# A hybrid decoder trunk on one core: the closing seven-product group of three SwiGLUs takes five blocks instead of four

## The chip, the cores and the metric

The kernel runs on one core of a Trainium2 chip. The core has a matrix engine (TensorE, here PE), a vector engine (VectorE, DVE), an activation engine (ScalarE, ACT), GpSimd (POOL) and a synchronisation engine (SyncE, SP). In this kernel SP and POOL issue nearly all of the DMA transfers, which the core's 16 DMA engines carry out. The metric is the time of one execution in microseconds (us).

## The reference

Two layers work on one sequence of 512 tokens with model width 1024, all in float32. Each layer has a SwiGLU, a mixing part (sliding-window attention beside a short convolution, with one combined input and one output projection) and a second SwiGLU. What matters here are the four SwiGLUs:

```python
D_MODEL = 1024
SEQ = 512
DEPTH = 2
D_FF = 2816
...
def swiglu(h, w_gate, w_up, w_down):
    return (jax.nn.silu(h @ w_gate) * (h @ w_up)) @ w_down
...
    for l in range(DEPTH):
        x = x + 0.5 * swiglu(rms_norm(x, ffn1_norm[l]), ffn1_wg[l], ffn1_wu[l], ffn1_wd[l])
        h = rms_norm(x, mix_norm[l])
        ...
        x = x + jnp.concatenate([attn_out, conv_out], axis=-1) @ w_out[l]
        x = x + 0.5 * swiglu(rms_norm(x, ffn2_norm[l]), ffn2_wg[l], ffn2_wu[l], ffn2_wd[l])
    return rms_norm(x, final_norm)
```

The down product (`@ w_down`) has the hidden width 2816 as its inner dimension, 1024 columns and 512 rows of tokens.

## The kernel before

**Precision.** Each float32 operand is split into a rounded part and what is left: `hi` is a cast on ACT (line 221), `lo = raw - hi` a subtraction on DVE (line 222), both in the type that PE multiplies at full rate. A product takes three matmuls: hi x hi, lo x hi, hi x lo. Weights arrive by DMA as tiles `raw_n` of two rows of 128 x 512 (shape 128 x 2 x 512, called 128x1024 in the profile, 512 KB) and become `wh_n` and `wl_n`. There are 8 buffers for raw tiles and 4 each for `wh` and `wl`; `take_split` asks for the split of the tile three ahead (`SPLIT_AHEAD`), and each split asks for a load four tiles further on (`LOAD_AHEAD`). Both wait for the buffer that comes round.

**A SwiGLU in blocks.** The hidden width is 11 blocks of 256. A list of stages tells in which order gate, up and down products are done: `p` and `w` make activations of one or two blocks, `u` those of block 10, `d` is a plain down product of the blocks named, `s` a group. The lists are `FIRST` (first SwiGLU of layer 0), `INNER` (second of layer 0, first of layer 1) and `LAST` (second of layer 1).

**A plain block** (`down`, line 383) multiplies one block's activations with its 2 weight rows: 4 row pieces of 128 tokens, 2 column halves of 512, 2 inner rows of 128, 3 matmuls each, so 48 matmuls of 128x512. Its results are added into the residual `x` by DVE (line 1372) or go on in banks that a group left open. In `INNER` the last two blocks have their own routine, `down_end` (line 422), which also feeds the next norm and takes one weight tile in other room (`wx`).

**A group** (`s`) takes four blocks and does seven products where plain multiplication has eight, after the seven-product scheme for 2 x 2 block matrices. Three objects take part:

- `plan` (function `seven`) puts ten weight tiles of the four blocks in line, some loaded with a second one added on top by an accumulating DMA that POOL issues, and orders seven forms of them (`FORMS`, or `EARLY` for the group at an end). Sums of tiles are made in `need_split`: on DVE as raw<-raw (line 249) or as a DMA of POOL (line 277).
- `Seven` makes the operands from the activations: b11, b21, b22 are the raw blocks (`fb..` tiles, 128x1024), t1 to t4 sums of them (`ft..` tiles). Each is split on ACT and DVE, but names listed in `far` take `split_far`: ACT writes the negative of the raw tile (line 227) and the rounded part (line 228), and POOL adds the raw tile by DMA (line 229).
- `share` runs the seven steps; a step is 2 weight tiles times 12 matmuls, so a group has 7 x 24 = 168. The accumulators are called x, y, w and z, here `x_s`, `y_s`, `w_s`, `z_s`, and go into `x` on DVE (line 1005).

The operands of the second group are made inside the steps of the first. `share` with `after` is the form for an end: it also drives the next norm, whose transposes (`xt`, line 705) stand between the last products.

**What sets the order.** A scheduler puts the instructions of each engine in a row; each engine works through its row in order and waits by semaphores. POOL issues its DMAs in order too, so what stands behind a waiting one waits with it. At the ends PE's row is written by hand (`by_hand`).

Of the kernel before, what the change touches and what calls it, by code (L numbers as in the profile page):

```python
# [8 lines left out]
F32 = mybir.dt.float32  # L9
# [7 lines left out]
P = 128  # L17
D = 1024
S = 512
# [50 lines left out]
    ((1, 1, -1), (0, 1, 1)), ((0, 1, 1),),  # L70
)
# [4 lines left out]
def trunk_kernel(  # L76
# [154 lines left out]
    def need_split(g):  # L231
        while state["split"] <= min(g, len(order) - 1):
# [3 lines left out]
            if what in (None, "wide", "room", "far"):  # L236
                need_raw(u if far else u + LOAD_AHEAD)
                raw = raw_of.pop(u)
            elif isinstance(what, tuple):

                what, h, how = what
                far = how == "far"
                last = {"a11": 0, "a12": 4, "s2": 2, "s3": 6, "s1": 2, "a22": 8, "s4": 4}[what]
                need_raw(u + h if far else u + max(last, 4) + h + LOAD_AHEAD)
                a11, s1, a12, s3, a22 = (raw_of.get(u + 2 * i + h) for i in range(5))
                if what == "s2":
                    late = state["late"] if h else None
                    with tc.issue_after(late) if late else nullcontext():
                        nc.vector.tensor_add(a11, a11, s1)  # L249
# [14 lines left out]
            if what == "room":  # L264
                hi, lo = both(f"wx_{n}", shape=(P, 2, 2, S))
            else:
                hi = wpool.tile(shape, F32R, tag="wh", bufs=4, name=f"wh_{n}")
                lo = wpool.tile(shape, F32R, tag="wl", bufs=4, name=f"wl_{n}")
# [4 lines left out]
            if isinstance(order[n][1], tuple):  # L273
# [13 lines left out]
                for i in done:  # L287
                    del raw_of[u + 2 * i + h]
            split_of[n] = (hi, lo)
            state["split"] += 1  # L290
            if far:

                with tc.issue_after(sent.ins):
                    need_raw(u + LOAD_AHEAD + (4 + h if isinstance(order[n][1], tuple) else 0))
# [110 lines left out]
    def down_end(acts, blocks, norm, open_):  # L405

        a, b = blocks
        held = []

        def tile_of(n):  # L410
            while len(held) <= n:
                held.append(take_split(min(SPLIT_AHEAD, 4 - len(held)))[1:])
            return held[n]

        def products(acc, t, n):
            tok = slice(t * P, (t + 1) * P)
# [1397 lines left out]
```

## Time and profile before

| what | us |
| --- | --- |
| median of 3 runs | 1635.62 |
| lowest and highest | 1635.52, 1637.23 |
| profiled execution | 1635.43 |
| its span | 1633.7 |
| PE busy | 1624.8 (99%) |
| DVE busy | 1304.0 (80%) |
| ACT busy | 1142.0 (70%) |
| POOL busy | 192.1 (12%) |

The span is the time from the first to the last record of the execution. Engines work side by side, so their busy times don't add up. In the rows of groups the columns are line, engine, operation, out<-in by the program's names, shape and count, then busy us in all and mean ns of one, then idle time before it and what ended it. In the table of stages each stretch is from:to in us, with the busy time of every engine, the granted clock of TensorE, the busy share of the 16 DMA engines and GB/s. The weight loads of the first SwiGLU's last three stages lie between 244 and 338 us.

### The profile page before, as it was taken

The page shows a single profiled execution, that of the slowest core. Times are in us where ns is not written, and L with a number is a line of the kernel's source. Part 1 is how long each engine was busy: PE and PEld are TensorE (multiplying, and loading weights), DVE is VectorE, ACT ScalarE, POOL GpSimd, SP SyncE. Part 2 cuts the span into 40 slices and gives each one's busy share as a digit, 9 for nine tenths or more (in the row PEclk, how much of TensorE's full clock was granted, in tenths as well). Part 3 has the DMA queues.
Part 4 walks back from the last instruction along what each step waited for, and adds up shares of the span by engine and source line. Part 5 has one row for each costly group of instructions (what it writes and reads, how often), then busy time and mean ns, then how long its engine had stood idle before and what let it go on. Part 6 is the DMA issues. An engine that isn't in the chain of part 4 may idle for free.

```text
span 1633.7 us, 21063 instructions
## 1 busy us (share of the span) xinstructions
PE 1624.8 (99%) x7544; PEld 1353.7 (83%) x7544; DVE 1304.0 (80%) x1718; ACT 1142.0 (70%) x1597; POOL 192.1 (12%) x172
## 2 busy tenths in 40 slices
PE   9999999999999999999999999999999999999998
PEld 7888888898888888888888888888988888888886
DVE  7987779878899867789688667887678987778885
ACT  7457777558867677786476777865597775777864
POOL 0011111100120111112001111110002101111111
PEclk9999999999999999999999999999999999999999
DMA  9379999934685788999737888997147857899992
GB/s 258 88 196 220 222 224 251 219 90 88 177 200 129 206 207 218 210 235 254 217 82 202 211 211 220 234 246 199 45 108 196 202 132 196 215 213 234 222 248 84
DMA packets 295292, 310.74 MB, mean 190 GB/s; under 512 B 116980, under 2 KB 179476, under 8 KB 295188
## 3 DMA queue, kind: packets, MB, share of 16 engines
q1 hardware_dynamic: 252660, 230.09, 48.7%
q0 software_dynamic: 41824, 78.65, 28.3%
q8 instruction: 59, 0.97, 0.2%
q10 hardware_dynamic: 704, 0.66, 0.1%
q14 instruction: 45, 0.37, 0.1%
HBM read 263.74 MB, written 2.10 MB: 163 GB/s over the span
## 4 chain that ended last, share of the span: by engine, by line
PE 93%; ACT 5%; DVE 1%; DMA 1%; issue 1%; SPq 0%; ACTq 0%; DVEq 0%
PE x L961 25%; PE y L961 13%; PE x_s L961 10%; PE w L961 6%; PE y_s L961 5%; PE up L1118 4%; PE down L383 3%; PE w_s L961 3%; PE acc L313 3%; PE acc L314 3%; PE acc L316 2%; PE acc L360 2%; PE x_m L961 1%; PE xt L705 1%; PE y_m L961 1%; ACT p L1589 1%
## 5 line engine op out<-in xcount | busy, mean ns | idle before, releaser
L222 DVE TENSOR_TENSOR wl<-raw,wh 128x1024 fp32r<-128x1024 f32 (+1 forms) x493 | 599.2, 1221 | 211.3 <-ACT wh L221 204.8
L221 ACT CAST wh<-raw 128x1024 fp32r<-128x1024 f32 (+1 forms) x493 | 511.7, 1044 | 300.3 <-PE y L961 37.5
L961 PE MATMUL x<-wh,ft 128*128 128x512 f32 x608 | 187.2, 389 | 0.0
L961 PE MATMUL y<-wh,ft 128*128 128x512 f32 x608 | 187.1, 389 | 0.0
L961 PE MATMUL x<-wh,fb 128*128 128x512 f32 x608 | 187.1, 389 | 0.0
L961 PEld LDWEIGHTS x<-wh,ft 128*128 128x128 f32 x608 | 114.2, 188 | 23.7
L961 PEld LDWEIGHTS x<-wh,fb 128*128 128x128 f32 x608 | 114.2, 188 | 23.7
L961 PEld LDWEIGHTS y<-wh,ft 128*128 128x128 f32 x608 | 114.1, 188 | 23.7
L961 PE MATMUL x<-wl,fb 128*128 128x512 f32 x304 | 118.3, 389 | 0.0
L961 PE MATMUL x<-wl,ft 128*128 128x512 f32 x304 | 118.3, 389 | 0.0
L961 PE MATMUL y<-wl,ft 128*128 128x512 f32 x304 | 118.3, 389 | 0.0
L1287 ACT COPY raw_a<-pt 128x1024 uint16<-128x1024 uint16 x76 | 103.3, 1360 | 17.9 <-DMA pt<-pl 17.8
L216 POOL DMA_DIRECT2D raw<-in_ffn_wu_dram x39 | 47.0, 1208 | 546.3 <-DMA raw<-in_ffn_wu_dram 351.4
L313 PE MATMUL acc<-hh,wh 128*128 128x512 f32 x240 | 94.0, 392 | 0.0
L961 PE MATMUL w<-wh,fb 128*128 128x512 f32 x304 | 93.6, 389 | 0.0
L314 PE MATMUL acc<-hl,wh 128*128 128x512 f32 x240 | 93.5, 390 | 0.0
L316 PE MATMUL acc<-hh,wl 128*128 128x512 f32 x240 | 93.4, 389 | 0.0
L961 PE MATMUL y_s<-wh,ft_s 128*128 128x512 f32 x256 | 78.8, 389 | 0.0
L961 PE MATMUL x_s<-wh,ft_s 128*128 128x512 f32 x256 | 78.8, 389 | 0.0
L249 DVE TENSOR_TENSOR raw<-raw,raw 128x1024 f32<-128x1024 f32 x58 | 70.5, 1219 | 9.1 <-DMA raw<-in_ffn_wd_dram 6.0
L216 POOL DMA_DIRECT2D raw<-in_ffn_wg_dram x39 | 46.8, 1206 | 235.2 <-DMA raw<-in_ffn_wu_dram 88.4
L961 PE MATMUL x_s<-wh,fb_s 128*128 128x512 f32 x240 | 74.0, 389 | 0.2 <-DVE x L1005 0.2
(370 smaller groups left out, 3431.7 us busy)
## 6 DMA issues: line engine op xcount, KB each, us to landing
raw<-in_ffn_wu_dram SPq DMA_DIRECT2D x120, 512.0 KB, 5.1
raw<-in_ffn_wd_dram SPq DMA_DIRECT2D x104, 512.0 KB, 6.9
raw<-in_ffn_wg_dram SPq DMA_DIRECT2D x80, 512.0 KB, 5.4
raw<-in_ffn_wu_dram POOLq DMA_DIRECT2D x39, 512.0 KB, 8.4
raw<-in_ffn_wg_dram POOLq DMA_DIRECT2D x39, 512.0 KB, 5.9
raw<-in_w_in_dram SPq DMA_DIRECT2D x36, 512.0 KB, 4.5
raw<-in_ffn_wd_dram POOLq DMA_DIRECT2D x32, 512.0 KB, 8.6
raw<-raw POOLq DMA_DIRECT2D x20, 512.0 KB, 8.9
```

What stands on the lines that cost most here:

```text
L216: nc.gpsimd.dma_start(out=r, in_=rows_of(*more), accum_op=ALU.add)
L221: cast = nc.scalar.copy(hi, raw)
L222: state["sub"] = eng.tensor_sub(lo, raw, f32(hi))
L249: nc.vector.tensor_add(a11, a11, s1)
L313: nc.tensor.matmul(acc, hi[:, k, :], rhs[k][0], start=k == first, stop=False)
L314: nc.tensor.matmul(acc, hi[:, k, :], rhs[k][1], start=False, stop=False)
L316: state["product"] = nc.tensor.matmul(acc, lo[:, k, :], rhs[k][0], start=False, stop=k == last)
L360: nc.tensor.matmul(accs[j][:, t * H : (t + 1) * H], w[:, k, :], x_, start=t + k + i == 0, stop=k == KC - 1 and i == 2, skip_group_check=True,)
L383: nc.tensor.matmul(acc, a[:, k, tok], w[:, k, :], start=i + k + n == 0 and fresh[t], stop=i == last and k == 1 and n == 2, skip_group_chec ...
L961: nc.tensor.matmul(accs[u], x_[:, 2 * h + k, tok], w[:, k, :], start=start and h + k + i == 0, stop=h + k == 2 and i == 2, skip_group_chec ...
L1118: nc.tensor.matmul(accs[t], x_[:, tok], w[:, k, :], start=j + k + i == 0, stop=j == 3 and k == 1 and i == 2,)
L1287: nc.scalar.copy(room.rearrange("p c (n z) -> p c z n", z=2)[:, :, z, :], turned[0][:, NT * z + 2 * c : NT * z + 2 * c + 2, :],)
```

## The change

In `FIRST` and `INNER` the closing group takes a fifth block. Four of its five blocks pair up as before; the fifth adds a single row of 128 to each side of the 2 x 2 scheme, so that each of the seven steps has 5 row tiles (2 + 2 + 1) instead of 4, and 30 matmuls. One plain block is left out in each: in `FIRST` the one of block 10 between the two groups, in `INNER` one of the closing two, while the other, block 1, stands between the groups. `LAST` does as before. With it come:

- one-row weight tiles (128x512) in the room `g2`, placed among the others by `THREES`; their splits use the same four buffers;
- one-row operands `fxb..` and `fxt..` (128x256), made by `make_extra` at the steps that `EXTRA` lists, with their own sums `sx`;
- the forms b11 and t1 of the closing group become far;
- the activations of the fifth block stay raw (`winograd`, `seventh`);
- `down_end` and the room `wx` go; the inner SwiGLUs close with `share` in its end form;
- the sends, joins and splits of one pair of blocks come at other ticks (`gap`, `start`, `part` at tick 60).

```diff
 FIRST = (
     ("p", 0), ("p", 1), ("d", (0,)), ("w", 2), ("d", (1,)), ("w", 4), ("w", 6), ("w", 8), ("u", 10),
-    ("s", 2), ("d", (10,)), ("s", 6),
+    ("s", (2, 4, None)), ("s", (6, 8, 10)),
 )
 INNER = (
-    ("p", 0), ("w", 1), ("d", (0,)), ("w", 3), ("w", 5), ("w", 7), ("w", 9), ("s", 1), ("s", 5),
-    ("d", (9, 10)),
+    ("p", 0), ("w", 1), ("d", (0,)), ("w", 3), ("w", 5), ("w", 7), ("w", 9), ("s", (3, 5, None)),
+    ("d", (1,)), ("s", (7, 9, 2)),
 )
-LAST = INNER[:-1] + (("d", (9, 10)),)
+LAST = INNER[:-3] + (("s", (1, 3, None)), ("s", (5, 7, None)), ("d", (9, 10)))
...
+PAIRS = ((0, 1), (2, 3), (4, 5), (6, 7), (8, 9))
+THREES = ((0, 1, 2), (3, 4, 10), (5, 6, 8), (7, 9, 13), (11, 12, 14))
+THREES_EARLY = ((0, 1, 2), (3, 4, 11), (5, 6, 8), (7, 9, 10), (12, 13, 14))
+EXTRA = (("b21+",), ("t1", "t2+"), ("b22", "t4", "t3+"), ("t1+", "t4+"), ("b22+",), (), ())
+EXTRA_EARLY = (
+    ("t3", "b21+"), ("t2", "t3+"), ("t4", "t1", "t2+"), ("b22", "t4+", "t1+"), ("b22+",), (), (),
+)
...
-            r = stock(f"raw_{n}", shape=(P, kc, wide * (2 if n in beside else 1)))
+            room = g2 if kc == 1 else stock
+            r = room(f"raw_{n}", shape=(P, kc, wide * (2 if n in beside else 1)))
             if n >= OPEN:
-                load(r, n, 0, kc)
+                with behind(state["load"] if kc == 1 else None):
+                    load(r, n, 0, kc)
...
-                need_raw(u + h if far else u + max(last, 4) + h + LOAD_AHEAD)
-                a11, s1, a12, s3, a22 = (raw_of.get(u + 2 * i + h) for i in range(5))
+                if at is PAIRS:
+                    need_raw(u + max(at[last][h], at[2][h]) + LOAD_AHEAD)
+                else:
+                    need_raw(u + at[last][h] + 2 * LOAD_AHEAD - 1)
+                a11, s1, a12, s3, a22 = (raw_of.get(u + at[i][h]) for i in range(5))
...
+        def make_extra(self, what):
+            if not self.extra:
+                return
+            t = g2(f"fx{what[:-1]}_{self.name}", F32R, (P, 2, H))
+            self.forms[what] = hi, lo = t[:, :1], t[:, 1:]
+            fresh = what in ("t2+", "t3+") and not self.more
+            if fresh:
+                t = g2(f"sx_{self.name}", F32, (P, 2, H))
+                self.more = t[:, :1], t[:, 1:]
+            split(hi, lo, self.source(what[:-1], self.extra, self.more, fresh))
...
+            end = 2 if ops.extra else 1
+            if step == 0:
+                ops.make("b11+")
+            for h in range(end + 1):
+                if h == 2:
+                    ops.make(operand + "+")
+                xh, xl = ops.forms[operand + "+" * (h == 2)]
...
+            if ops.extra:
+                ops.make(*(EXTRA_EARLY if after else EXTRA)[step])
+            elif not soon:
                 ops.make(*[chains[n][1] for n in {1: (4,), 2: (6, 5)}.get(step, ())])
...
+            start = 6 + 2 * gap
+            if then == "s" and stages[-1][0] == "s":
+                gap, start = 1, 10
             plan = [(1 + n, send, n) for n in range(NT)]
...
         def shared(b):
-            return Seven([raw_act(b), raw_act(b + 2)], room_form, f"s_{whole}_{b}", far=("b22",))
+            lo, hi, x_ = b
...
+            far = ("b22",) if x_ is None else ("b11", "t1", "b22")
+            return Seven(full, room_form, f"s_{whole}_{lo}", far=far, extra=extra)
```

How the rows of the engines change at three places, all in the closing group of the first SwiGLU, which is `s_0_6` in the names (`s_0_2` is the opening group). The number after `wh_`, `wl_` or `raw_` is that of the weight tile, and the last number only tells tiles apart.

First PE, where the one-row operand fxb21 is used first. The rows before have the end of the second step of the closing group and the start of the third:

```order
L961 MATMUL w_s_0_2_0_2300<-wl_94_2635,fb21_s_0_6_2468 128x512
L961 MATMUL w_s_0_2_1_2301<-wh_94_2634,fb21_s_0_6_2468 128x512 x2
L961 MATMUL w_s_0_2_1_2301<-wl_94_2635,fb21_s_0_6_2468 128x512
L961 MATMUL w_s_0_2_1_2301<-wh_94_2634,fb21_s_0_6_2468 128x512 x2
L961 MATMUL w_s_0_2_1_2301<-wl_94_2635,fb21_s_0_6_2468 128x512
L961 MATMUL y_s_0_6_0_2718<-wh_95_2652,ft3_s_0_6_2506 128x512 x2
L961 MATMUL y_s_0_6_0_2718<-wl_95_2653,ft3_s_0_6_2506 128x512
L961 MATMUL y_s_0_6_0_2718<-wh_95_2652,ft3_s_0_6_2506 128x512 x2
```

Now, at the end of the two-row part of the second step:

```order
L944 MATMUL w_s_0_2_1_2297<-wh_93_2587,fb21_s_0_6_2549 128x512 x2
L944 MATMUL w_s_0_2_1_2297<-wl_93_2588,fb21_s_0_6_2549 128x512
L944 MATMUL y_s_0_6_0_2690<-wh_95_2627,ft3_s_0_6_2619 128x512 x2
L944 MATMUL y_s_0_6_0_2690<-wl_95_2628,ft3_s_0_6_2619 128x512
L944 MATMUL y_s_0_6_0_2690<-wh_95_2627,ft3_s_0_6_2619 128x512 x2
L944 MATMUL y_s_0_6_0_2690<-wl_95_2628,ft3_s_0_6_2619 128x512
L944 MATMUL y_s_0_6_1_2691<-wh_95_2627,ft3_s_0_6_2619 128x512 x2
L944 MATMUL y_s_0_6_1_2691<-wl_95_2628,ft3_s_0_6_2619 128x512
L944 MATMUL y_s_0_6_1_2691<-wh_95_2627,ft3_s_0_6_2619 128x512
L944 MATMUL w_s_0_2_0_2296<-wh_94_2607,fxb21_s_0_6_2624 128x512
L944 MATMUL w_s_0_2_1_2297<-wh_94_2607,fxb21_s_0_6_2624 128x512
L944 MATMUL y_s_0_6_1_2691<-wh_95_2627,ft3_s_0_6_2619 128x512
```

The w chain of wh_92 and wh_93 leaves off, the first matmuls of the t3 chain on wh_95 come ahead, and then the one-row products of fxb21 with wh_94.

DVE before, at the second tile of the closing group:

```order
L222 TENSOR_TENSOR ft4_s_0_6_2714<-sums_s_0_6_2507,ft4_s_0_6_2714 128x1024
L1372 SCALAR_TENSOR_TENSOR x3_92<-down_90_3_2595,x3_92 128x512
L222 TENSOR_TENSOR wl_94_2635<-raw_74_2532,wh_94_2634 128x1024
L762 TENSOR_TENSOR raw_a_0_6_1854<-raw_a_0_6_1854 128x4x256
L222 TENSOR_TENSOR wl_95_2653<-raw_75_2534,wh_95_2652 128x1024
L1005 SCALAR_TENSOR_TENSOR x0_89<-x_s_0_6_0_2632,x0_89 128x512
L222 TENSOR_TENSOR ft1_s_0_6_2762<-raw_a_0_6_1854,ft1_s_0_6_2762 128x1024
L1005 SCALAR_TENSOR_TENSOR x0_89<-x_s_0_6_1_2633,x0_89 128x512
L222 TENSOR_TENSOR wl_96_2673<-raw_76_2537,wh_96_2672 128x1024
```

DVE now, from the third step's first tile:

```order
L231 TENSOR_TENSOR wl_95_2628<-raw_74_2489,wh_95_2627 128x1024
L261 TENSOR_TENSOR raw_68_2339<-raw_68_2339,raw_71_2482 128x1024
L231 TENSOR_TENSOR wl_96_2646<-raw_76_2528,wh_96_2645 128x1024
L748 TENSOR_TENSOR sums_s_0_6_2620<-sums_s_0_6_2620,raw_a_0_8_2258 128x1024
L231 TENSOR_TENSOR wl_97_2664<-raw_77_2561,wh_97_2663 128x512
L746 TENSOR_TENSOR raw_a_0_6_1854<-raw_a_0_6_1854 128x4x256
L231 TENSOR_TENSOR fxb21_s_0_6_2624<-a_0_10_2226,fxb21_s_0_6_2624 128x256
L742 TENSOR_TENSOR sx_s_0_6_2686<-a_0_10_2226 128x256
L231 TENSOR_TENSOR ft4_s_0_6_2744<-sums_s_0_6_2620,ft4_s_0_6_2744 128x1024
```

The subtraction into raw_a, which makes t1, now stands between wl_97 and fxb21, and the split of the whole t1 (ft1) is gone from the row.

POOL before, from the far form of the opening group:

```order
L229 DMA fb22_s_0_2_2381<-raw_a_0_4_1544 128x4x256
L216 DMA raw_71_2487<-in_ffn1_wd_dram 128x2x512
L216 DMA raw_72_2511<-in_ffn1_wd_dram 128x2x512
L216 DMA raw_75_2534<-in_ffn1_wd_dram 128x2x512
L216 DMA raw_76_2537<-in_ffn1_wd_dram 128x2x512
L229 DMA fb22_s_0_6_2758<-raw_a_0_8_2262 128x4x256
```

POOL now:

```order
L238 DMA fb22_s_0_2_2377<-raw_a_0_4_1544 128x4x256
L225 DMA raw_70_2424<-in_ffn1_wd_dram 128x2x512
L238 DMA fb11_s_0_6_2462<-raw_a_0_6_1854 128x4x256
L225 DMA raw_71_2482<-in_ffn1_wd_dram 128x2x512
L225 DMA raw_74_2489<-in_ffn1_wd_dram 128x2x512
L225 DMA raw_76_2528<-in_ffn1_wd_dram 128x2x512
L225 DMA raw_77_2561<-in_ffn1_wd_dram 128x512
L225 DMA raw_78_2564<-in_ffn1_wd_dram 128x512
```

The far copy of fb11 stands between the accumulating loads of raw_70 and raw_71, and two of the later accumulating loads are of one row.

More of the change, by code (lines that the diff above doesn't have):

```diff
@@ L509, in ffn @@
                         if half == 0 or not end or stages is not LAST:
-                            room = end and stages is not LAST and (half, k) == (0, b[0])
-                            order.append((u, "room" if room else "wide"))
+                            order.append((u, "wide"))
         for l in range(DEPTH):
@@ L1365, in ffn @@
                 return
[L1366 to L1368 removed]
+            for n, (t, o, acc) in enumerate(down(acts, b, open_)):
+                if w and any(acc is z for z in w):
                     continue
```

179 lines of the change are left out of this document (76 added, 103 removed).

## The prediction

> **What bounds the kernel now.** First the page's table of busy time, with the time of the TensorE (PE), VectorE (DVE), ScalarE (ACT) and GpSimd (POOL), and then the table of PE's waits.
>
> ```profile
> PE 1624.8 (99%) x7544; PEld 1353.7 (83%) x7544; DVE 1304.0 (80%) x1718; ACT 1142.0 (70%) x1597; POOL 192.1 (12%) x172
> ```
> ```profile
> PE idle L150 <- DVE warm L805: 1.2, 1, 1.2
> PE xt L824 <- DMA x<-in_x_dram: 0.3, 1, 0.3
> PE x_s L961 <- DVE x L1005: 0.2, 1, 0.2
> PE y_m L961 <- ACT wh L221: 0.2, 1, 0.2
> ```
>
> PE is busy for 99% and its four waits add up to 1.9 us of 1633.7. So a matmul that goes away is worth its whole price, as long as nothing that PE waits for becomes late. The price comes from the chain of waits through the first SwiGLU's last groups (start, length, work):
>
> ```profile
> 282.30 5.44 PE x_s L961 x24
> 287.74 2.72 PE w_s L383 x12
> 290.46 2.72 PE x_s L383 x12
> 293.18 2.72 PE y_s L383 x12
> 295.90 2.72 PE down L383 x12
> 298.62 5.44 PE x_s L961 x24
> ```
>
> 24 matmuls of 128x512 take 5.44 us, 12 take 2.72: 0.2267 us each, in a group and in a plain block alike (the four L383 rows are the plain block of layer 0's first SwiGLU, 10.88 us for 48). Third, the busy time of each engine by stage. The columns are PE, PEld, DVE, ACT, POOL, granted TensorE clock, DMA share, GB/s; the stages are the first SwiGLU's opening group, its plain block and its closing group, then the two groups and the closing plain pair of layer 0's second SwiGLU.
>
> ```profile
> 244.20:287.70 43.50, 43.50 (x215) 36.93 (x214) 42.32 (x47) 32.02 (x35) 7.86 (x7) 1.00 0.99 248
> 287.70:298.60 10.90, 10.90 (x50) 9.03 (x49) 9.24 (x10) 4.97 (x6) 2.60 (x3) 1.00 0.63 155
> 298.60:338.50 39.90, 39.90 (x187) 33.17 (x185) 34.07 (x46) 23.24 (x35) 2.97 (x3) 1.00 0.85 205
> 721.20:759.30 38.10, 38.10 (x169) 31.55 (x169) 34.14 (x37) 29.20 (x33) 7.40 (x8) 1.00 1.03 251
> 759.30:797.40 38.10, 38.10 (x169) 31.54 (x169) 33.36 (x34) 22.33 (x23) 4.92 (x5) 1.00 1.03 263
> 797.40:820.90 23.50, 23.50 (x113) 19.64 (x112) 13.40 (x22) 12.30 (x25) 2.40 (x2) 1.00 0.53 122
> ```
>
> In the first SwiGLU's opening group DVE is 97% busy (42.32 of 43.5) and the DMA engines 99%: PE does not wait, but nothing is spare. Both recover in the plain block behind it (DMA 0.63), which the change takes away. In the inner SwiGLUs the groups run with DVE at 88 to 90% and a full DMA, and recover at the end (DVE 57%, DMA 0.53).
>
> **The change part by part.**
>
> *Matmuls.* Each of the three SwiGLUs had two groups of 7 x 24 = 168 and plain blocks of 48 (one in the first; two closing ones in the others). Its closing group now has 7 x 30 = 210 and one plain block is gone: 168 + 48 - 210 = 6 matmuls fewer. 3 x 6 x 0.2267 = 4.08 us off PE, all of it on the path.
>
> *DVE and ACT work.* It grows. The durations, from the groups by shape between 240 and 345 us:
>
> ```profile
> L222 DVE TENSOR_TENSOR wl<-raw,wh 128x1024 fp32r<-128x1024 f32 (+1 forms) x493 | 599.2, 1221 | 211.3 <-ACT wh L221 204.8
> L762 DVE TENSOR_TENSOR raw_a<-raw_a 128x1024 f32<-128x1024 f32 x2 | 2.4, 1217 | 0.0
> L222 DVE TENSOR_TENSOR a<-up,a 128x512 fp32r<-128x512 f32 x2 | 1.4, 684 | 0.0
> L1193 DVE TENSOR_TENSOR up<-y,u 128x256 f32<-128x256 f32 x2 | 0.8, 415 | 0.0
> L221 ACT CAST a<-up 128x512 fp32r<-128x512 f32 x2 | 1.2, 617 | 0.8 <-DVE up L1196 0.8
> ```
>
> (the first is the page's row). Consecutive DVE instructions overlap by about 0.08 us, as two rows of the timeline show: the next starts 1.14 us after one that lasts 1.22.
>
> ```profile
> 289.56 1.22 DVE L222 TENSOR_TENSOR wl<-raw,wh 128x1024 fp32r<-128x1024 f32 x1
> 290.70 1.22 DVE L249 TENSOR_TENSOR raw<-raw,raw 128x1024 f32<-128x1024 f32 x1
> ```
>
> So a step costs DVE 1.14, 0.60 or 0.335 us by size. Added over the kernel: 21 weight splits of 128x512 (12.6), 21 activation splits and 12 small sums of 128x256 (11.1), 3 weight sums and 2 net bank evictions of 128x512 (3.0). Removed: 4 weight splits, 2 into the old closing room, and the 6 forms that go to POOL, all 128x1024 (12 x 1.14 = 13.7). That is 13.0 us more. In the first SwiGLU, from the split of the group's last opening tile to the next norm, the order has 3.9 us more on DVE. The two stages behind 287.7 held 9.24 + 34.07 = 43.3 us of DVE in 50.8; they will hold 47.2 in 49.4 (50.8 less 1.36), 96%. That is as dense as the stage before it, which ran without a wait, so the mean fits; the order decides.
>
> The tight place is the one-row form fxb21 of the first SwiGLU. Weight tiles have four buffers, so the cast into wh_97 waits for PE's last matmul on wh_93, and DVE's row then reads wl_97, the 128x1024 subtraction into raw_a, fxb21. From release to use: 0.617 (ACT) + 0.60 + 1.14 + 0.415 = 2.77 us. In that time PE has one last matmul on wl_93 and the 10 of the t3 chain that stand ahead of the first fxb21: 11 x 0.2267 = 2.49 us. It lacks 0.3 us; with the handing over from PE to ACT to DVE to PE I take 0.4. In the inner SwiGLUs a 128x256 sum stands in the place of the 128x1024 one: 0.617 + 0.60 + 0.335 + 0.415 = 1.97 against the same 2.49, so cover of 0.5 us is left; I take 0.05 each. Bounds: 0 if ACT's part overlaps other work and only DVE's own row counts (2.15), and 1.4 us if one further 128x1024 row (1.14) is in the way.
>
> *Far forms.* fb11 and t1 of the three-wide group leave DVE: ACT writes the negative and POOL adds by DMA. t1 comes late and has several groups of cover (5.44 us each). In the inner SwiGLUs fb11 has the plain block's 10.88 us as cover, above the 9.5 that such a copy took (row below): 0, or the 0.4 of the first one if that block's loads take the queue. fb11 is the first operand of the closing group. In the first SwiGLU, POOL issues it behind the accumulating load of raw_70, which waits for its base. The nearest rows: the far copy of the opening group, then two accumulating loads, each alone (KB, us to landing), then the issue of the first of these two and DVE's wait for the second.
>
> ```profile
> fb_s<-raw_a POOLq DMA_DIRECT2D x1, 512.0 KB, 9.5
> raw<-in_ffn_wd_dram POOLq DMA_DIRECT2D x1, 512.0 KB, 9.8
> raw<-in_ffn_wd_dram POOLq DMA_DIRECT2D x1, 512.0 KB, 13.1
> ```
> ```profile
> 280.35 1.19 POOL L216 DMA_DIRECT2D raw<-in_ffn_wd_dram  x1 [10.86 <-DMA raw<-in_ffn_wd_dram]
> 295.31 1.23 DVE L249 TENSOR_TENSOR raw<-raw,raw 128x1024 f32<-128x1024 f32 x1 [1.66 <-DMA raw<-in_ffn_wd_dram]
> ```
>
> Before, the first accumulate of this kind left at 280.35; its base was the fifth load of the next blocks, and is now the fourth with one of half size ahead. At 248 GB/s 512 KB takes 2.11 us, so 1.5 loads earlier is 3.2 us, 277.2; fb11 follows some 1.2 us later, at 278.4. With the fast queue's 9.5 us it lands at 287.9, with 13.1 at 291.5. PE wants it at 287.7. The stall is 0.2 to 3.8 us; 0 if the base lands sooner. I take 0.4, near the row of the same copy.
>
> The Trainium skill (DMA: Bandwidth & Descriptors, "Anatomy of one DMA — SWDGE (gpsimd) path") fits one such DMA as 2.0 us plus bytes over 436e3. As an estimate from that page, 512 KB lands in 3.2 us, so that fb11 would be there near 282, this term would be 0 and the sum 0.4 us lower. The rows above, 9.5 to 13.1 us on a busy queue, don't bear it out.
>
> *DMA volume.* SP and POOL together issued 19 units of 512 KB for the first SwiGLU's plain block and closing group; they will issue 23 (four one-row loads too small to be whole, three accumulates more, two far copies more, two plain loads fewer). 4 x 2.11 = 8.4 us. The three stages had 0.01 x 43.5 + 0.37 x 10.9 + 0.15 x 39.9 = 10.5 us of free DMA time, less 1.36 for the shorter span: 9.1. So it just fits, all of it in the two later stages. SP's own row only has more and smaller loads in it, in the order in which their tiles are split; its issues wait for buffers as before. The next tile at risk is the accumulated raw_74: PE uses its split at 287.7 + 54 x 0.2267 = 299.9, and cast and split (1.05 and 1.22 us before) want it near 297.6. I take 0.1 us (bounds 0 and 4, two units late). In the inner SwiGLUs the plain block of 10.88 us now stands between the two full groups, which gives five units of recovery ahead of the closing group; I put that at 0.
>
> *Ends.* The inner SwiGLUs closed with their own routine of plain products, and now close as the first one does. Both ends run on PE without a gap, transposes (xt) and the last products in turn, first the end of the first SwiGLU, then the old inner one:
>
> ```profile
> 331.26 1.37 PE z_s L961 x6
> 332.63 0.87 PE xt L705 x8
> ```
> ```profile
> 813.68 0.87 PE xt L705 x8
> 814.55 2.74 PE down L422 x12
> ```
>
> 12 products in 2.74 and 6 in 1.37 cost the same each: 0, bounds -0.3 and +0.6 (both inner ends).
>
> *A wait that may go.* In layer 1 one PE wait lies at the seam between the two groups, where the plain block now goes.
>
> ```profile
> 1116.20 0.39 PE L961 MATMUL y_s<-wl,ft_s 128*128 128x512 f32 x1
> 1116.78 0.70 PE L961 MATMUL x_s<-wh,fb_s 128*128 128x512 f32 x2 [0.20 <-DVE x L1005]
> ```
>
> The starts are 0.58 apart, 0.35 more than a matmul. It vanishes or comes again: -0.2.
>
> *Sum.* -4.08 + 0.4 (fxb21) + 0.1 (inner forms) + 0.4 (fb11) + 0.1 (raw_74) + 0 - 0.2 = -3.3 us. The profiled execution took 1635.43 us (span 1633.7), 0.2 under the median of the runs, 1635.62. 1635.4 - 3.3 = 1632.1 us.
>
> **The rivals.**
>
> *Everything is covered.* The DVE density of 97% ran without a wait in the opening group, and ACT's row may reach the cast of wh_97 without delay. Then the gain is the full 4.08 and the seam's 0.35: 1631.0 to 1631.4 us.
>
> *The one-row chains stall in all three.* Each closing group loses about 0.5 us at fxb21 and again where the 128x512 splits make a slot turn twice as often. Against it stands the cover of 0.3 us in the inner ones. 6 x 0.5 = 3 us with nothing regained: 1635.43 - 4.08 + 3.0 = 1634.4, within 0.2%.
>
> *The first SwiGLU's DMA runs late (the other side).* Without the plain block nothing drains the backlog ahead of the closing group: a backlog that made one accumulate take 13.1 us and made DVE wait 1.66 us even with the plain block there. If fb11 lands 3.8 us late and raw_74 is then still two units (4.2 us) behind, PE loses 8.0: 1635.4 - 4.08 + 8.0 - 0.2 = 1639.2 us. It decides from 4 us of stall, about two units of 2.11. Against it: DVE's 1.66 us at 295.3 reached no PE wait of the table, and a stall of PE gives the queue that time back, so that the two delays don't fully add.
>
> *No real change* would need PE to have been paced by something else; 1.9 us of waits exclude it.
>
> **How the numbers follow.** About 0.2%, 3.3 us, is what a measurement of this kernel can tell from no change: 1632.35 and 1638.9 against the median. My sum lies just on the faster side. Chances: full cover 0.26; the sum as forecast with small stalls 0.33, of which 0.2 is faster and 0.13 is not; chains stalling everywhere 0.17, no measurable change; late DMA 0.24, of which 0.13 ends above 1638.9, 0.02 is faster by half-hidden stalls, and 0.09 within the bound. So faster 0.48, same 0.39, slower 0.13. The range goes from 1630.9 (full cover, seam regained, 0.1 for the spread of runs) to 1638.0, which leaves out the worse half of the late transfers.
>
> **What the profile after would show.** PE's 128x512 matmuls down by 18. A PE wait at the first fxb21 of the first SwiGLU, at 299.9 + 10 x 0.2267 = 302.2 us, of about 0.4 us, released by DVE; none over 0.2 us in the two inner ones. A PE wait near 287.7 released by the DMA of fb_s, under 1 us. DVE at 94 to 97% and DMA at 0.9 or more from 287.7 to 337. The 1116 us wait smaller or gone. The granted clock stays at 1.00. The prediction is wrong if a PE wait on a DMA in the first SwiGLU exceeds 2 us, if DVE is late by more than 1 us in an inner closing group, or if the new inner ends leave PE waiting for the norm.

## The result, and the profile after

The changed kernel takes 1646.28 us (median of 5, 1641.4 to 1647.41) against 1635.9 us before (median of 5, 1635.52 to 1637.41): a ratio of 1.0056 with a 95% interval of 1.004 to 1.0073. It is slower, by about 9 us (6.5 to 11.9 by the interval), and its executions lie further apart than those of the kernel before. The profiled one took 1645.55 us, 10.1 us more than that of before.

The page's busy times show that the work did change as counted. PE has 18 instructions fewer (7544 before), DVE 10.6 us more.

```profile
PE 1625.5 (99%) x7526; PEld 1351.1 (82%) x7526; DVE 1314.6 (80%) x1761; ACT 1156.9 (70%) x1635; POOL 207.7 (13%) x187
```

PE is still "99%", and yet it holds the difference. Its busy time did not fall by 4 us, but rose by 0.7, and it has new waits. The table of PE's waits after:

```profile
PE x_s L944 <- DMA fb_s<-raw_a: 5.3, 1, 5.3
PE w_s L944 <- DVE fxb_s L231: 1.9, 2, 1.0
PE y_s L944 <- DVE wl L231: 1.2, 2, 0.6
PE idle L157 <- DVE warm L787: 1.2, 1, 1.2
PE xt L806 <- DMA x<-in_x_dram: 0.6, 1, 0.6
PE w_s L944 <- ACT fxb_s L230: 0.6, 2, 0.3
PE y_m L944 <- ACT wh L230: 0.2, 1, 0.2
```

The first row is the far copy of fb11 in the first SwiGLU. The rows with `fxb_s` and `wl` occur twice each, once in each inner SwiGLU. The stages around the first wait (columns as before: PE, PEld, DVE, ACT, POOL, granted clock, DMA share, GB/s):

```profile
287.90:293.70 5.80, 0.48 (x3) 0.06 (x2) 4.76 (x6) 2.09 (x2) 1.21 (x1) 0.87 1.15 275
293.70:299.00 5.30, 5.30 (x13) 4.13 (x14) 0.00 (x0) 0.64 (x1) 1.76 (x2) 0.50 1.13 212
```

PE stands for nearly all of the first stretch. In the second it is "busy" for all of it, but with 13 matmuls in 5.3 us, where the usual 0.2267 us would allow 23: the granted clock is 0.50. These 13 matmuls took 2.4 us more than at the usual pace, half of the 4.8 us by which the busy time lies above what 18 matmuls fewer would leave. The Trainium skill (TensorE: Matmul & The Clock Gate, "What's actually happening") says that an idle window of about 3.4 us halves this clock and that it takes a busy one to bring it back; the two stretches agree with that, and in other runs (last section) waits of 3.2 and 3.3 us already halved it.

PE's row and the transfers of that place (KB, us to landing, each issued alone: the accumulating load of raw_70, then fb11's copy, then the accumulating load of raw_71, then the two loads of the next norm's gain):

```profile
287.95 0.39 PE L944 MATMUL x_s<-wh,fb_s 128*128 128x512 f32 x1
293.65 0.79 PE L944 MATMUL x_s<-wh,fb_s 128*128 128x512 f32 x1 [5.32 <-DMA fb_s<-raw_a]
```
```profile
raw<-in_ffn_wd_dram POOLq DMA_DIRECT2D x1, 512.0 KB, 9.0
fb_s<-raw_a POOLq DMA_DIRECT2D x1, 512.0 KB, 13.7
raw<-in_ffn_wd_dram POOLq DMA_DIRECT2D x1, 512.0 KB, 16.2
gain<-in_mix_norm_dram SPq DMA_DIRECT2D x2, 256.0 KB, 10.5
```

fb11's copy was issued at 279.91 and landed at 293.6. The gain loads were issued at 280.70 and 281.22, into the same crowd; before the change they went at 245.96 and 246.51, some 35 us earlier.

The inner loss is in ACT's row. In the first inner SwiGLU:

```profile
788.26 1.05 ACT L230 CAST wh<-raw 128x1024 fp32r<-128x1024 f32 x1
789.21 1.05 ACT L236 ACTIVATE fb_s<-raw_a 128x1024 fp32r<-128x1024 f32 x1
790.16 1.03 ACT L237 CAST fb_s<-raw_a 128x1024 fp32r<-128x1024 f32 x1
791.10 1.56 ACT L230 CAST wh<-raw 128x1024 fp32r<-128x1024 f32 x2
792.57 0.40 ACT L230 CAST fxb_s<-raw_a 128x256 fp32r<-128x256 f32 x1
```

The first cast is that of wh_240. Then come the two instructions of the far form of b22, which PE first uses at 821.15, four steps later, and only then wh_241, wh_242 and fxb21. PE waits for what is behind them:

```profile
793.02 0.73 PE L944 MATMUL w_s<-wh,fxb_s 128*128 128x512 f32 x2 [0.30 <-ACT fxb_s L230]
794.73 0.50 PE L944 MATMUL w_s<-wh,fxb_s 128*128 128x512 f32 x1 [0.97 <-DVE fxb_s L231]
```

To compare runs I add up PE's lost time in three stretches: for every pair of neighbouring matmuls, the distance of their starts in the trace less the usual one (0.227 us for 128x512). This counts waits and slow matmuls alike. It is of the profiled execution alone.

| run | median us (lowest to highest) | profiled us | lost at 280 to 312 | at 765 to 800 | at 1080 to 1125 |
| --- | --- | --- | --- | --- | --- |
| before | 1635.9 | 1635.43 | 0 | 0 | 0.4 |
| changed | 1646.28 (1641.4 to 1647.41) | 1645.55 | 8.1 | 3.0 | 2.9 |

The account closes: 8.1 + 3.0 + 2.9 - 0.4 (the wait of before at 1116, which is gone) - 4.1 (18 matmuls) = 9.5 of the 10.1 us.

### The profile page after: what moved, and what is told of

Read it like the earlier page. It is cut to its first block, busy times and chain, and to the rows that moved or that the text cites. A ratio compares the mean times of both kernels' runs of the same rounds, so it can differ in the third digit from the quotient of the medians.

```text
span 1643.7 us, 21164 instructions
## 1 busy us (share of the span) xinstructions
PE 1625.5 (99%) x7526; PEld 1351.1 (82%) x7526; DVE 1314.6 (80%) x1761; ACT 1156.9 (70%) x1635; POOL 207.7 (13%) x187
## 4 chain that ended last, share of the span: by engine, by line
PE 89%; ACT 5%; DVE 3%; DMA 2%; issue 1%; SPq 0%; POOL 0%; ACTq 0%; DVEq 0%; POOLq 0%
PE x L944 25%; PE y L944 13%; PE x_s L944 9%; PE w L944 6%; PE y_s L944 5%; PE up L1108 4%; PE down L392 4%; PE acc L322 3%; PE acc L323 3%; PE acc L325 2%; PE w_s L944 2%; PE acc L369 2%; PE x_m L944 1%; PE z_s L944 1%; PE xt L668 1%; PE y_m L944 1%
## 5 line engine op out<-in xcount | busy, mean ns | idle before, releaser
L231 DVE TENSOR_TENSOR wl<-raw,wh 128x1024 fp32r<-128x1024 f32 (+2 forms) x510 | 608.1, 1197 | 231.2 <-ACT wh L230 227.7
L230 ACT CAST wh<-raw 128x1024 fp32r<-128x1024 f32 (+2 forms) x510 | 520.7, 1026 | 309.7 <-PE y L944 41.9
L261 DVE TENSOR_TENSOR raw<-raw,raw 128x1024 f32<-128x1024 f32 (+1 forms) x61 | 72.4, 1190 | 5.3 <-DMA raw<-in_ffn_wd_dram 4.0
L225 POOL DMA_DIRECT2D raw<-in_ffn_wd_dram x38 | 44.6, 1176 | 237.0 <-DMA raw<-in_ffn_wd_dram 102.7
```

Of the source, the lines that this page charges most:

```text
L225: nc.gpsimd.dma_start(out=r, in_=rows_of(*more), accum_op=ALU.add)
L230: cast = nc.scalar.copy(hi, raw)
L231: state["sub"] = eng.tensor_sub(lo, raw, f32(hi))
```

## The experiments

The theory after the result: (A) in the first SwiGLU fb11's far copy is late, and the wait is long enough to halve the clock; (C) in the inner ones the far form of b22 stands in ACT's way. Rivals: (B) the DMA engines are behind as a whole, so that something else would be late in fb11's place; (D) the one-row tiles cost what the buffers or DVE lack. Lost times are given as first / inner of layer 0 / inner of layer 1, in the stretches of the table, shifted where a run was.

**One SwiGLU kind at a time.** In `first_alone` the inner SwiGLUs are those of before, with `down_end`; in `inner_alone` the first is.

```diff
 # first_alone
 INNER = (
-    ("p", 0), ("w", 1), ("d", (0,)), ("w", 3), ("w", 5), ("w", 7), ("w", 9), ("s", (3, 5, None)),
-    ("d", (1,)), ("s", (7, 9, 2)),
+    ("p", 0), ("w", 1), ("d", (0,)), ("w", 3), ("w", 5), ("w", 7), ("w", 9), ("s", (1, 3, None)),
+    ("s", (5, 7, None)), ("d", (9, 10)),
...
 # inner_alone
-    ("s", (2, 4, None)), ("s", (6, 8, 10)),
+    ("s", (2, 4, None)), ("d", (10,)), ("s", (6, 8, None)),
```

> Changed: only the first SwiGLU closes with five blocks; the inner two are as before the change, with their closing plain pair. If the losses add up: 1635.4 - 1.4 (6 matmuls) + 8.0 (wait and slow matmuls at 288 us) = 1642.0 us. If the other parts of the change bring on the loss in the first SwiGLU: about 1634.

> Changed: the first SwiGLU keeps its two groups of four blocks and the plain block of block 10; the two inner ones are as in the changed kernel. If the losses of the three SwiGLUs add up: 1635.4 - 2.7 (12 matmuls) + 5.8 (the inner waits) - 0.35 (the wait at 1116 us) = 1638.2 us, and the 8.0 us near 288 us are absent. If the inner waits are brought on by the first SwiGLU's delay, 1633 us.

Measured: 1644.45 us (1639.68 to 1647.08, ratio 1.0054, 1.0037 to 1.0071) and 1645.01 us (1640.82 to 1645.41, ratio 1.0055, 1.0037 to 1.0073). Lost in the profiled executions (1639.68 and 1640.82 us, each the fastest of its kernel): 6.0 / 0 / 0 and 0 / 3.6 / 3.5. The losses sit where the changed blocks are, and neither kind needs the other. The first profiled time fits the added-up losses (1635.4 - 1.4 + 6.0 = 1640.0); the second is 1.4 us above them (1635.4 - 2.7 + 7.1 - 0.4 = 1639.4). But the medians lie 4 to 5 us above these executions, so others lose more; each kind alone costs as much by its median as both together. The 1642.0 us expected of the first SwiGLU and the 1638.2 us expected of the inner ones were both missed.

**fb11 on DVE in the first SwiGLU.**

```diff
-            far = ("b22",) if x_ is None else ("b11", "t1", "b22")
+            far = ("b22",) if x_ is None else ("t1", "b22") if first else ("b11", "t1", "b22")
```

> Changed: in the first SwiGLU only, fb11 of the closing group is split on DVE, as b21 is, instead of by ACT and a POOL DMA. Theory A (the far copy of fb11 lands 5.5 us late, and after so long a wait PE runs at half its rate for some 5 us): the wait of 5.3 us at 288 us and the slow matmuls behind it go, 8.0 us together; DVE gets 1.14 us more and may be up to 1 us late at its first one-row form. 1645.6 - 8.0 + 0 to 1 = 1637.6 to 1638.6 us. Rival B (the DMA engines are simply behind without the plain block, and the next late tile takes the place): a PE wait of 3 us or more for a later weight tile, and 1641 us or more.

Measured: 1647.31 us (1643.35 to 1647.81), no better. Lost: 2.5 / 3.9 / 8.7 (profiled 1647.67). The wait at 288 us and the slow clock behind it are gone, 8.1 became 2.5, as theory A has it. What is left is a wait of 2.4 us at the first fxb21, released by ACT. ACT's row there:

```profile
300.66 1.05 ACT L230 CAST wh<-raw 128x1024 fp32r<-128x1024 f32 x1 [3.03 <-DMA raw<-in_ffn_wd_dram]
301.62 1.04 ACT L230 CAST ft_s<-sums_s 128x1024 fp32r<-128x1024 f32 x1
302.56 0.62 ACT L230 CAST wh<-raw 128x512 fp32r<-128x512 f32 x1
304.15 1.06 ACT L236 ACTIVATE ft_s<-raw_a 128x1024 fp32r<-128x1024 f32 x1 [0.96 <-DVE raw_a L746]
305.11 0.39 ACT L230 CAST fxb_s<-a 128x256 fp32r<-128x256 f32 x1
```

The cast of wh_96 waits 3.03 us for the accumulated raw_76, and fxb21's own small cast stands behind it and behind t1's far form. What the kernel gained here it lost in layer 1's inner SwiGLU, which the edit doesn't touch. The tile of the transposes (`pt`) there, this run and the kernel before:

```profile
  DMA pt<-pl: 10.8, 1
DMA to landing us min/median/max: 13.1/14.3/14.9
```
```profile
  DMA pt<-pl: 3.4, 1
DMA to landing us min/median/max: 4.1/5.6/7.1
```

The transposes that turn the last activations landed after 14 us, with the inner fb11's far copy in flight over the same time (issued 1069.4, landed 1085.8). ACT waited 10.8 us to copy them out, the casts of the weights behind that copy were late, and PE stood for 3.2 us and ran at half the clock behind it. In the profiled execution of the changed kernel, with the same copy beside them (9.8 us), the same transposes took 7.8 to 9.3 us and PE did not wait. So these two executions differ by how late these transfers were; why, the traces don't show.

**The far copy earlier.**

```diff
-                    soon = {4: ("b11",), 6: ("b21",)}
+                    soon = {2 if first else 4: ("b11",), 6: ("b21",)}
```

> Changed: in the first SwiGLU only, the far form of fb11 is asked for after the opening group's third step instead of its fifth, so that POOL issues it ahead of the accumulating load of raw_70. The bytes are the same. Theory A, with the issue behind that load as the cause: fb11 lands some 6 us sooner, near 282, the wait and the slow matmuls go, 8.0 us: 1637.6 us. Rival B (too many bytes in this stretch): what is behind fb11 lands as late as fb11 did, a PE wait of 3 us or more stays there or moves to a weight tile, 1641 us or more.

Measured: 1649.23 us (1642.22 to 1652.08). Lost: 8.4 / 5.0 / 5.3. fb11 was issued at 271.9, landed at 287.5 after 15.6 us, and the wait for it is gone. In its place stands one of nearly the same size at 300.6 us for the split of raw_74, whose accumulating load landed at 303.95 (299.6 in the changed kernel); PE's table and ACT's row:

```profile
PE y_s L944 <- ACT wh L230: 4.2, 1, 4.2
```
```profile
304.05 1.04 ACT L230 CAST wh<-raw 128x1024 fp32r<-128x1024 f32 x1 [7.13 <-DMA raw<-in_ffn_wd_dram]
```

This is what rival B expects. The load that raw_74 is added onto took 14.0 us here (issued at 280.07, landed at 294.08) and 5.8 us in the changed kernel, so that POOL could issue the accumulating load only at 294.95, not at 285.03. Together with the run before it, theory A holds for the place of the wait, and B for its cause: one transfer fewer took 5.6 us off this stretch (8.1 to 2.5), the same transfer earlier took off nothing.

**The gain loads later.** They are asked for at the closing group's fourth step.

```diff
-            if final and after:
+            if final and after and what != "s":
                 after.begin()
...
+            if after and step == 3 and after.gain is None:
+                after.begin()
```

> Changed: the changed kernel, with the gain loads asked for at the fourth step of the closing group and nothing else. In the first SwiGLU they started at 280.7 us while the far copy of fb11 was in flight until 293.6. Theory G: fb11 lands about 2 us sooner, the wait falls from 5.3 to about 3.3 us and the slow matmuls behind it mostly go, 8.0 becomes 3.5 to 5 us: 1641 to 1642.5 us. If fb11's landing is set by the accumulating loads ahead of it in its own queue: no change, 1645.6 us.

Measured: 1645.16 us (1642.91 to 1647.08), no change; the 1641 to 1642.5 us of theory G were missed. Lost: 5.5 / 4.8 / 2.8. fb11's wait fell from 5.3 to 3.6 us, which is the size expected but for another reason in the main: the copy was issued at 278.75, 1.2 us sooner, and took 13.2 us instead of 13.7, while the gain loads of the changed kernel had started only behind the copy's issue. The slow clock came behind the wait still, 1.7 us, and at 774 us, at the seam to the inner closing group, there is a wait of 1.2 us that the changed kernel's profile lacks. The gain of 2.6 us in the first SwiGLU is in the trace, not in the times.

**b22 held back in the inner SwiGLUs.**

```diff
+                late = what == "b22" and self.extra and "s_0_" not in self.name
+                with behind(state["cast"] if late else None):
+                    (split_far if what in self.far else split)(hi, lo, src)
...
-    ("t3", "b21+"), ("t2", "t3+"), ("t4", "t1", "t2+"), ("b22", "t4+", "t1+"), ("b22+",), (), (),
+    ("t3", "b21+"), ("t2", "t3+"), ("b22", "t4", "t1", "t2+"), ("t4+", "t1+"), ("b22+",), (), (),
```

> Changed: in the two inner SwiGLUs, the far form of b22 (two ACT instructions of 1.05 us) is asked for one step earlier but held back on ACT until the cast of the latest weight tile, so that it no longer stands between the casts of the third step's first and second tile. Theory C (those two instructions make the casts late, and with them the one-row form fxb21): of 3.0 and 2.8 us of PE time lost near 790 and 1117 us at least 2 us each go, 1645.6 - 4 = 1641.6 us or less. Rival D (the four buffers of the weight splits, which turn more often with one-row tiles, or DVE's own work): the waits stay above 2 us each, 1644 us or more.

Measured: 1647.01 us (1640.88 to 1652.39); profiled 1640.88. Lost: 6.1 / 2.1 / 1.0. In the trace the inner losses fall by 0.9 and 1.9 us, and by 1.6 without a seam wait of 0.7 at 775 us. That speaks for C, less than the 2 us each that were expected. The median doesn't show it, and 1641.6 us was missed: the late copy of the first SwiGLU is still there, and this trace is of the fastest of five executions by 4.5 us. The waits of the table above for `fxb_s` (1.9 and 0.6 us) have become these:

```profile
PE w_s L946 <- DVE wl L231: 0.7, 2, 0.5
PE w_s L946 <- DVE fxb_s L231: 0.6, 2, 0.3
```

The other traces bear C out. In the six kernels with five blocks in the inner SwiGLUs and b22 not held back, PE's starts at fxb21 are 1.0 to 1.15 us too far apart in each of the twelve inner closing groups; in the six with b22 held (two of them with fxb21 earlier too), in none by more than 0.5 us.

**fb11 on DVE in the inner ones.** The first SwiGLU is as before the change; `far` leaves out b11.

```diff
-    ("s", (2, 4, None)), ("s", (6, 8, 10)),
+    ("s", (2, 4, None)), ("d", (10,)), ("s", (6, 8, None)),
...
-            far = ("b22",) if x_ is None else ("b11", "t1", "b22")
+            far = ("b22",) if x_ is None else ("t1", "b22")
```

> Changed: the first SwiGLU as before the change; the inner ones with five blocks and fb11 on DVE, but b22 not held back and the gain loads where the change has them. Theory J (two causes: the far copy of fb11 competes with the transposes and loads ahead of the closing group and makes the executions differ by 5 us; the two ACT instructions of b22 cost 2 us in each group): the losses that stay are those of b22's place, 1.5 to 2.5 us in each closing group, so 1635.4 - 3.1 + 3 to 5 + 0.8 = 1636 to 1638 us, and no execution above 1640. If the spread has another cause, executions of 1644 us come again, as with the inner SwiGLUs alone; if ACT's row was crowded by fb11 as much as by b22, below 1635.5 us.

Measured: 1637.28 us (1634.14 to 1639.58, 10 executions; ratio 1.0006, 0.9996 to 1.0015), against 1645.01 with the far copy. None of ten is above 1640 us. Lost: 0 / 1.1 / 2.8, at fxb21 again. The time is what theory J expected (1636 to 1638 us). The largest part of what the inner SwiGLUs cost is this one far form, a copy and one more ACT instruction, and without it the executions near 1645 us, three of four in `inner_alone`, don't come. The transposes go with it: ACT waits 3.7 to 10.8 us for them in each inner SwiGLU of the traces in which fb11 is far, and 0.9 to 4.4 us where it is split on DVE. That the copy itself, and not its ACT instruction, makes the slow executions is inferred; the trace of `inner_alone` is of its fast execution.

**Both mends, and more.** `dve_and_held` has fb11 on DVE in all three and b22 held back; `dve_held_gain` the gain loads later besides; `all_early21` also asks for fxb21 together with b11; `all_t1_dve` also takes t1 from the far forms. `inner_mended` is `dve_held_gain` with the first SwiGLU as before the change. The holding of b22, the later gain loads and that first SwiGLU are edited as in the diffs above; only the rest is shown here.

```diff
 # dve_and_held, dve_held_gain, all_early21, inner_mended
-            far = ("b22",) if x_ is None else ("b11", "t1", "b22")
+            far = ("b22",) if x_ is None else ("t1", "b22")
 # all_t1_dve
-            far = ("b22",) if x_ is None else ("b11", "t1", "b22")
+            far = ("b22",)
 # all_early21, all_t1_dve
-                ops.make("b11+")
+                ops.make("b11+", "b21+")
```

> Changed: fb11 is split on DVE in all three SwiGLUs, and b22 is held back in the inner two. Theory E (transfers of POOL between SBUF tiles compete with loads and transposes, and each stall is a landing that comes late; less of them helps everywhere): 2.5 us lost near 303 us as in the run with fb11 on DVE, 1.0 to 1.3 us in each inner closing group as in the run with b22 held, and the transposes near 680 and 1075 us land as fast as before the change (about 4 us, at most 7): 1635.4 - 4.1 - 0.35 + 2.5 + 2.3 + 0.7 (small ones) = 1636.5 us, with a spread of 2 us. Rival F (the five-block groups themselves ask for more than DMA and DVE give): waits of 3 us or more somewhere in each execution, 1641 us or more.

> Changed: as the run before, and the two loads of the next norm's gain (256 KB each) are asked for at the closing group's fourth step instead of at its start, so that they no longer stand between its weight loads. Theory G (in the first SwiGLU the weight tiles behind the gain loads are late for the 2.1 us that 512 KB take): of the 2.5 us near 303 us at least 1.5 go, 1635.0 us. Rival: the loads are late for another reason, 1636.5 us as without it.

> Changed: the first SwiGLU as before the change (two groups of four blocks and the plain block), the inner ones with five blocks, fb11 on DVE, b22 held back and the gain loads later. If the two mends take away the inner losses whole: 1635.4 - 2.7 (12 matmuls) - 0.35 + 0.8 (what was left of waits in the run with both mends) = 1633.2 us, and the 1645 us of three of the four executions with the inner SwiGLUs alone don't come again (spread below 2 us). If they need the first SwiGLU's form for it: 1636 us or more.

> Changed: as the run with fb11 on DVE, b22 held back and the gain loads later, and the one-row form b21 of the fifth block (fxb21) is asked for together with b11 at the closing group's start, in all three SwiGLUs. In ACT's row its cast then stands ahead of the casts of the third step's weight tiles, which wait for the accumulated raw_76. Theory H (the 2.6 us near 303 us are this order: fxb21's cast stands behind a cast that waits for a load): the wait goes or falls below 0.7 us, and the time from 1633.5 to 1631 to 1632 us. Rival I (the loads are late for PE itself): the wait moves to the weight tile of raw_76 or raw_77 with 2 us or more, 1633 to 1634 us.

> Changed: as the run beside it, and t1 too is split on DVE in all three SwiGLUs, so that of the far forms only b22 is left, as before the change. One transfer and one ACT instruction fewer in each closing group, one DVE step of 1.14 us more. If transfers are what is short: 0.5 to 1.5 us faster than the run beside it. If DVE is what is short in the closing groups: 0.5 to 3 us slower, with PE waits on DVE.

| run | median us (lowest to highest, executions) | ratio to before (95%) | profiled us | lost first / inner 0 / inner 1 |
| --- | --- | --- | --- | --- |
| dve_and_held | 1636.71 (1633.46 to 1642.23, 10) | 1.0004 (0.9993 to 1.0015) | 1637.98 | 6.0 / 0.5 / 0.1 |
| dve_held_gain | 1633.51 (1632.09 to 1637.24, 10) | 0.9986 (0.9976 to 0.9995) | 1637.24 | 2.8 / 0.1 / 2.6 |
| inner_mended | 1635.18 (1633.99 to 1638.12, 10) | 0.9988 (0.9979 to 0.9997) | 1633.99 | 0 / 0.1 / 0.1 |
| all_early21 | 1634.72 (1633.23 to 1638.61, 12) | 0.9988 (0.998 to 0.9997) | 1634.52 | 0 / 1.1 / 1.2 |
| all_t1_dve | 1632.07 (1631.28 to 1633.67, 4) | 0.9967 (0.9954 to 0.998) | 1631.28 | 0 / 0.1 / 0.1 |

The last three ran beside a kernel before of 1636.65 us, the first two beside one of 1635.99, so across the two the ratios are to be compared.

`dve_and_held` met the 1636.5 us expected, in part by luck: in its trace 6.0 us are lost in the first SwiGLU where 2.5 were expected, 0.6 in the inner ones where 2.3 were, and the executions spread by 8.8 us, not 2. So E holds for the inner SwiGLUs; in the first one the wait of 3.3 us at fxb21 is the 3 us that rival F named. Moving the gain loads took 3.2 us off the median, about twice the least that was expected, though alone it had brought nothing. The trace of `dve_held_gain` is of the slowest of its ten executions, so its losses are more than the usual ones, and whether the wait at 303 us fell in the others isn't known. Asking for fxb21 earlier took the wait at 303 us away in the trace (2.8 to 0), as theory H has it, but not from the ratio: waits of 0.7 to 0.8 us for splits of weights came in the inner SwiGLUs, and the 1631 to 1632 us were missed. Whether they are due to the earlier form or differ from execution to execution is open. `inner_mended` expected 1633.2 us and a spread below 2 us: its profiled execution lost 0.2 us in the three stretches and took 1633.99, its median is 1635.18 and its spread 4.1.

`all_t1_dve` is the fastest version, 0.33% below the kernel before (four executions; the interval just touches that of `all_early21`). It has one far copy in each group, as the kernel before, and does 3 splits more on DVE than `all_early21`. PE has no wait in any of the three closing groups; its whole table, and the stretches in which the changed kernel stood and then crawled:

```profile
PE idle L157 <- DVE warm L789: 1.2, 1, 1.2
PE xt L808 <- DMA x<-in_x_dram: 0.4, 1, 0.4
```
```profile
287.70:293.70 6.00, 6.00 (x28) 4.95 (x28) 6.00 (x8) 5.12 (x6) 1.20 (x1) 1.00 1.11 256
293.70:299.00 5.30, 5.30 (x25) 4.40 (x24) 4.55 (x6) 1.68 (x3) 3.71 (x4) 1.00 1.01 167
```

DVE works through the first of them without a gap and PE does not wait for it, so DVE was not what was short. Whether t1's far form had cost by its transfer or by its second ACT instruction, this run doesn't separate: both went. The profiled 1631.28 us are 4.15 less than before: the 18 matmuls, whole.

## Why the prediction was wrong, point by point

The forecast was 1632.1 us, faster, in a range of 1630.9 to 1638.0. Measured were 1646.28 us, slower. The prediction's first sign of being wrong came: a PE wait on a DMA in the first SwiGLU of more than 2 us.

*Matmuls, -4.08 us.* Right in count and price. The run with no waits left took 4.15 us less than before.

*The far copy of fb11, +0.4 us (bounds 0.2 to 3.8).* This is the first step that failed. Its issue was put at 278.4 us (it was 279.91) and its landing time at the 9.5 us of the copy before it, with 13.1 as the other end (it was 13.7), so the wait of 5.3 us lies 1.5 us past the worse end. Of two rows far apart the wrong one was taken: the copy with 9.5 us was issued at 268.19, the load with 13.1 at 282.14, nearer to where fb11 would stand. The share of the DMA engines would not have told them apart: it was 1.04 from 268.2 to 277.7 and 0.86 from 280 to 295. And a wait was priced as a wait: the half clock behind it added 2.6 us. Together 8.1 us, a size that only the late-DMA rival named (8.0). That rival had 0.24, and its size is luck: it added a late raw_74 where the changed kernel shows the slow clock.

*DMA volume, +0.1 us.* The count of four units more was right (22 whole and 8 half transfers between 262 and 340 us without the gain and the next weights, 22 whole ones before), and so was a DMA share above 0.9. The mistake was to read free time from a mean share: 9.1 us free for 8.4 wanted over three stages, where the wait and the slow matmuls fall into the first 12 us behind the seam. Nor is 1.00 the most that this share can show: the prediction's own rows have 1.03, and these 12 us 1.13 to 1.15. The early copy shows the shortage, since its gain was paid back by raw_74. The gain loads (246 us before, 281 after) weren't counted at all: no edit names them, and only SP's row shows that they moved.

*Inner forms, +0.05 us each.* The second step that failed: 3.0 and 2.9 us. The chain from a free buffer to fxb21 had 0.617 us for ACT, as if ACT were waiting for it. The far forms were said to leave DVE for POOL, and their two ACT instructions (1.05 and 1.03 us) were not laid into ACT's row; b22's stood exactly there. Holding them back took 0.9 and 1.9 us off in the trace, and with fb11's ACT work and copy away as well 0.5 and 0.1 us are left. (The rival of stalls in all three puts the inner cover at 0.3 us, where the prediction's own sum has 0.5.)

*fxb21 of the first SwiGLU, +0.4 us.* The place was right, the size too small, and the chain another one. In the changed kernel fb11's wait hides it. With that gone it is 2.4 to 3.3 us, and what is late is not the buffer of wh_97 but ACT's row: fxb21's cast stands behind the cast of raw_76 and behind t1's far form. With fxb21 asked for earlier the wait is gone.

*Inner fb11, 0.* The plain block's 10.88 us were named as cover for PE, and they do cover it. But the transposes are late beside it, which PE feels through ACT, and of the runs with the inner fb11 on DVE only `dve_and_held` has executions above 1640 us (two of ten). The other transfers that the copy meets were left out.

*Seam, -0.2, and ends, 0.* In the profiled execution the seam's wait at 1116 us is gone, and no PE wait lies at the ends. Both right there, and small; three other runs have a seam wait of 1.2 to 1.7 us in one inner SwiGLU or both.

*The clock stays at 1.00.* Wrong, as said: 0.50 over 5.3 us of running.

Not settled: why the medians of `first_alone` and `inner_alone` lie 4 to 5 us above their profiled executions. Late transposes with the slow clock behind them are shown in one trace; that they make up the rest in the others is inferred from the runs with the inner fb11 on DVE.

## What to carry to other kernels

Work that is taken from a busy engine by giving it to DMA must be paid in the stretch in which it lands, with the transfer times of that stretch; in a crowded one the mean share of the DMA engines doesn't tell, and here a transfer brought forward made another late. "Far" work has a part on the issuing side too: lay every instruction that it leaves (here two on ACT) into the row of its engine, between the very instructions that the next consumer waits for. And where PE is the bound, count a wait of more than about 3 us with the half-speed matmuls that follow it.

## What the runs showed of the hardware

In these runs the half clock has an edge between 2.7 and 3.2 us. After PE waits of 2.4 and 2.7 us (fb11 on DVE, and with the gain loads later; by the distance of the starts) the granted clock stayed at 1.00; with those of 3.2, 3.3, 3.8, 4.3, 4.5 and 5.5 us it fell to 0.50 for a while. Two rows show both sides, the stretch behind a wait of 2.7 us and that behind one of 3.3 (`dve_held_gain`, then `dve_and_held`):

```profile
305.90:311.00 5.10, 5.10 (x22) 4.13 (x23) 5.10 (x9) 5.07 (x8) 1.21 (x1) 1.00 1.05 284
```
```profile
307.40:313.00 5.60, 5.51 (x17) 4.31 (x18) 5.51 (x9) 5.57 (x10) 1.29 (x1) 0.70 1.10 230
```

0.70 over 5.6 us is a clock of 1.00 up to 308.9 us, 0.50 for the next 3.4 and 1.00 again: it fell when PE had been running for 1.4 us. In the changed kernel it was 0.50 from 292.2 to 299.0 us, of which PE stood for the first 1.5. So the slow clock doesn't begin where the wait ends. It lasted 3.4 us in four of these traces and 6.8 us in three.

Three transfers of 512 KB that POOL accumulates, issued within 1.5 us, took 9.0, 13.7 and 16.2 us, against a median of 8.8 for its accumulating loads of the down weights over the changed kernel. Transposes that took 4.1 to 7.1 us before took 7.8 to 9.3 in the changed kernel and 13.1 to 14.9 in one other run, both with such a copy beside them. An engine that waits for the one or the other passes the delay on to whatever stands behind it in its row.
